# A hybrid decoder layer on one core: xBC, z and most gates as pairs of tiles in block products, with the scan between them

## The chip, the cores and the metric

The kernel runs on one core of a Trainium2 chip. Its engines work side by side, each on its own list of instructions in order: TensorE (matmuls), VectorE, ScalarE, GpSimd, and SyncE, which issues the DMAs. The metric is the device time of one execution in microseconds (us). Shorter is better.

## The reference, cut to what matters

All arrays are float32, x is 1024 tokens by 1024 channels, and one layer is computed.

```python
h = rms_norm(x, g_pre)
proj = jnp.einsum('bsd,dc->bsc', h, w_in)              # 1024 -> 12576 columns
(q, k, v, z_a, u, v_s, z_s, z_m, xbc, dt_raw, gate_logits) = jnp.split(proj, _split_points(), axis=-1)
y_att = sliding_window_attention(q, k, v, sinks, rel_bias) * jax.nn.silu(z_a)     # 16 heads of 64, window 128
y_sg = chunked_spatial_gate(u, v_s, sg_ln_g, sg_ln_b, sg_w, sg_b) * jax.nn.silu(z_s)
y_ssm = ssd_mixer(z_m, xbc, dt_raw, conv_w, conv_b, dt_bias, a_log, d_skip, ssm_norm_g)
gates = jax.nn.sigmoid(gate_logits.reshape(bsz, seq, N_BRANCHES, D_MODEL))
merged = gates[:, :, 0] * (y_att @ w_br_att) + gates[:, :, 1] * (y_sg @ w_br_sg) + gates[:, :, 2] * (y_ssm @ w_br_ssm)
return x + rms_norm(merged @ w_out, g_post)
```

The mixer `ssd_mixer` first runs a causal convolution of four taps and a silu over xbc (3072 channels: 2048 of x, 512 of B, 512 of C), and then, for each of 4 groups of 8 heads, a scan over 8 chunks of 128 tokens: inside a chunk, products of C and B weighted by decays; between chunks, a state of 128 by 512. Its output is multiplied by silu(z_m) (2048 channels) and normalised by group.

## The kernel before, in words

Each float32 operand of a large matmul is kept as a high and a low part, and three matmuls (high times high, high times low, low times high) make one product. A weight tile is loaded as `raw`, ScalarE rounds it to `whi`, VectorE subtracts to get `wlo` (`load_w`).

Most of the projection is made by `ct_unit`: one tile of 128 output channels for all 1024 tokens, in two halves of 512 tokens, each 8 steps over the input channels times three matmuls of 512 columns. `Stream.fill` puts pieces of such units into TensorE's order between the steps of other work; TensorE's order is the order of the program, the other engines' orders are set by a scheduler.

The stages are: the norm of x and a first unit; for each scan group g, six `conv_unit` tiles (xBC), then the 8 chunks of `Mix` with gate and z tiles as filler (from about 100 to 770 us); the attention with its q and z_a tiles; then u and z_s and twelve of the 24 gate tiles as pairs (to about 1400 us); the four quarters of the branch products (`br_unit`); and the output product.

The pairs are made by `PairStream`. It takes two tiles of output channels and the two halves of the tokens as a 2 by 2 block matrix, and makes it in seven block products in place of eight (twelve matmuls of 512 columns each). It needs sums of weight blocks (T1 to T4, on GpSimd, `ts`), sums of blocks of h (S1, S2 and S4, made once ahead of the stage), and sums of the products (u2, u3, u4 and the four output blocks, on VectorE out of PSUM and on GpSimd, `tp`). It prepares the operands of four products ahead.

A chunk in `Mix` has a part `local` (B and C and x of the chunk through TensorE; decays `seg`, `m` by ScalarE and VectorE), a part `scan` (the matmuls `po` with the state, `pn` for the new state, `pd` inside the chunk, then y on VectorE and GpSimd) and `sums`, which adds the squares of y over channels with a matmul. `decay` loads the decay rows two chunks ahead. The tiles xg, bc and z2 of a whole group stay in SBUF. The inverse norms of all chunks are made from `ssum` after the last group (a power on GpSimd, L622) and transposed after the units for k and q (L680).

In the branch stage `load_y` brings the y tiles back from DRAM; those of the first quarter wait for memory that the pairs' operands held.

## Time and profile before

| | |
|---|---|
| median of 3 runs | 1873.94 us (1871.6 to 1877.67) |
| the profiled execution's own time | 1872.69 us |
| its span, first to last instruction | 1871.0 us |
| mean granted TensorE clock | 0.988 |
| DMA | 192.85 MB, mean 103 GB/s |

The profile lists for each engine how long it was busy within the span, and for groups of instructions what ended the idle time in front of them. A wait of an engine that is not the bottleneck costs nothing by itself.

### The profile page before, as it was taken

Reading aid. Unit: us, or ns where it says so; the run is one execution under the profiler, and the core shown is the slowest. Engines: PE = TensorE matmul, PEld = TensorE weight load, DVE = VectorE, ACT = ScalarE, POOL = GpSimd, SP = SyncE. Lnnn points to the kernel's source line nnn. Section 1 sums busy time; section 2 is a strip of 40 time slices with the busy share of each in tenths; the row PEclk is TensorE's granted clock in tenths of the full one; section 3 lists DMA queues with packets and bytes.
Section 4 is the critical chain, followed back from the end, with each engine's and each line's share of the span. In section 5 each row is a group of like instructions: output and inputs, shape, how many; then the busy total and the mean of one; then the engine's idle time right before and its main releaser. Section 6 shows DMA issues by size and latency. Waiting matters only on the chain. (4 is left out here: it accounts for less than half of the span.)

```text
span 1871.0 us, 24800 instructions
## 1 busy us (share of the span) xinstructions
PE 1809.9 (97%) x9481; PEld 1529.9 (82%) x9481; DVE 1128.5 (60%) x1596; ACT 715.5 (38%) x1519; POOL 552.6 (30%) x552
## 2 busy tenths in 40 slices
PE   7999999999999999999999979999997999999998
PEld 6888778878878887888888978888885888888898
DVE  5446756675667557466666587766877243534424
ACT  5344454355436435356555433333233021212121
POOL 1000420240043015236665557554555200000000
PEclk9999999999999999999999989999998999999999
DMA  6211341342134124311111213322346453524303
GB/s 224 80 53 51 124 136 46 99 121 83 52 109 145 46 73 152 119 46 46 49 42 57 91 54 119 121 94 94 101 152 240 143 180 101 192 92 136 99 24 135
DMA packets 100662, 192.85 MB, mean 103 GB/s; under 512 B 9376, under 2 KB 55744, under 8 KB 100416
## 3 DMA queue, kind: packets, MB, share of 16 engines
q1 hardware_dynamic: 100544, 191.28, 31.5%
q8 instruction: 74, 1.21, 0.3%
q14 instruction: 44, 0.36, 0.1%
HBM read 152.83 MB, written 38.42 MB: 102 GB/s over the span
## 5 line engine op out<-in xcount | busy, mean ns | idle before, releaser
L106 PE MATMUL ps_mm<-h,whi 128*128 128x512 f32 x1104 | 436.3, 395 | 0.1
L108 PE MATMUL ps_mm<-h,wlo 128*128 128x512 f32 x1104 | 430.1, 390 | 0.0
L107 PE MATMUL ps_mm<-h,whi 128*128 128x512 f32 x1104 | 430.0, 389 | 0.0
L88 ACT CAST whi<-raw 128x1024 fp32r<-128x1024 f32 (+1 forms) x119 | 124.1, 1044 | 336.7 <-PE ps_mm L107 323.5
L108 PEld LDWEIGHTS ps_mm<-h,wlo 128*128 128x128 f32 x1104 | 207.2, 188 | 43.9
L106 PEld LDWEIGHTS ps_mm<-h,whi 128*128 128x128 f32 x1104 | 207.4, 188 | 43.5 <-issue 2.2
L107 PEld LDWEIGHTS ps_mm<-h,whi 128*128 128x128 f32 x1104 | 207.6, 188 | 40.7
L89 DVE TENSOR_TENSOR wlo<-raw,whi 128x1024 fp32r<-128x1024 f32 (+1 forms) x117 | 158.2, 1353 | 117.5 <-ACT whi L88 117.5
L106 PE MATMUL ps_mm<-y,whi 128*128 128x512 f32 x512 | 200.8, 392 | 11.1 <-ACT y L962 11.1
L107 PE MATMUL ps_mm<-y,whi 128*128 128x512 f32 x512 | 200.6, 392 | 2.0 <-DVE y L963 2.0
L108 PE MATMUL ps_mm<-y,wlo 128*128 128x512 f32 x512 | 200.1, 391 | 0.0
L552 POOL TENSOR_TENSOR y<-xg,dsk 128x512 f32<-128x512 f32 x32 | 40.5, 1276 | 390.0 <-issue 225.5
L493 DVE SCALAR_TENSOR_TENSOR acc<-xr,wcv,acc 128x512 f32<-128x512 f32 x144 | 111.4, 773 | 40.5 <-ACT acc L491 37.1
L106 PEld LDWEIGHTS ps_mm<-y,whi 128*128 128x128 f32 x512 | 96.9, 189 | 32.3 <-ACT y L962 11.9
L79 POOL TENSOR_TENSOR rso<-rso,mhalf_row 128x1 f32<-128x1 f32 x8 | 4.4, 552 | 401.0 <-DVE rso L78 401.0
L107 PEld LDWEIGHTS ps_mm<-y,whi 128*128 128x128 f32 x512 | 96.8, 189 | 23.1 <-DVE y L963 3.2
L985 DVE SCALAR_TENSOR_TENSOR tm<-gld,ps_mm 128x512 f32<-128x512 f32 x48 | 33.0, 687 | 134.6 <-PE ps_mm L108 134.6
L108 PEld LDWEIGHTS ps_mm<-y,wlo 128*128 128x128 f32 x512 | 96.8, 189 | 19.9
L131 PE MATMUL ps_mm<-whi,h 128*128 128x256 f32 (+1 forms) x256 | 81.6, 319 | 11.3 <-ACT whi L88 7.8
L528 ACT ACTIVATE seg<-seg,acs 128x128 f32<-128x128 f32 x256 | 80.4, 392 | 23.2 <-DMA seg<-acs_dr 22.2
L735 ACT ACTIVATE p<-s,mx 128x129 f32<-128x129 f32 x128 | 50.0, 392 | 96.3 <-DVE mx L731 96.3
L132 PE MATMUL ps_mm<-whi,h 128*128 128x256 f32 (+1 forms) x256 | 80.2, 313 | 1.8 <-DVE h L373 1.8
(236 smaller groups left out, 3753.8 us busy)
## 6 DMA issues: line engine op xcount, KB each, us to landing
seg<-acs_dr SPq DMA_DIRECT2D x32, 512.0 KB, 4.7
raw<-in_w_br_dram SPq DMA_DIRECT2D x32, 512.0 KB, 4.2
yraw<-y_dr SPq DMA_DIRECT2D x32, 512.0 KB, 5.3
gld<-gate_dr SPq DMA_DIRECT2D x32, 512.0 KB, 3.4
raw<-in_w_xbc_dram SPq DMA_DIRECT2D x24, 512.0 KB, 3.6
raw<-in_w_zm_dram SPq DMA_DIRECT2D x16, 512.0 KB, 3.5
y_dr<-y SPq DMA_DIRECT2D x32, 256.0 KB, 2.2
raw<-in_w_zu_dram SPq DMA_DIRECT2D x16, 512.0 KB, 3.5
```

The costliest lines, as they stand in the source:

```text
L88: A.copy(hi, raw)
L89: eng.tensor_tensor(lo, raw, hi.bitcast(F32), op=ALU.subtract)
L106: T.matmul(ps, lhsT=whi[:, ks], rhs=rhs(0, kt, half), start=kt == 0, stop=False)
L107: T.matmul(ps, lhsT=whi[:, ks], rhs=rhs(1, kt, half), start=False, stop=False)
L108: T.matmul(ps, lhsT=wlo[:, ks], rhs=rhs(0, kt, half), start=False, stop=kt == KT - 1)
L131: T.matmul(o, lhsT=lhs(0, kt, tt), rhs=whi[:, ks], start=kt == 0, stop=False)
L132: T.matmul(o, lhsT=lhs(1, kt, tt), rhs=whi[:, ks], start=False, stop=False)
L493: V.scalar_tensor_tensor(acc, xr[:, k + f0:k + f0 + 512], wcv[:, ti, k:k + 1], acc, op0=ALU.mult, op1=ALU.add)
L528: A.activation(seg[:, j, :], seg[:, j, :], AF.Relu, scale=-1.0, bias=acs[:, c, g * 8 + j:g * 8 + j + 1])
L552: G.tensor_tensor(d["y"], xg[g][:, :, cs], col(dsk, g), op=ALU.mult)
L735: A.activation(p[:, k, :], s4[:, k, :], AF.Exp, bias=mx[:, k:k + 1], accum_out=den[:, k:k + 1])
L985: V.scalar_tensor_tensor(tm, gt[0][:, fs], 1.0, ps, op0=ALU.add, op1=ALU.mult)
```

## The change

Attention comes first. Then one `PairStream` makes the xBC tiles (12 pairs), z (8 pairs), 22 of 24 gate tiles (11 pairs, one of them at the end) and the u and z_s tiles (8 pairs, as before). The scan's chunks stand between its products. As pairs come out of blocks and no longer stay for a whole group, the outputs go to DRAM (`x_dr`, `bc_dr`, `z_dr`), and each chunk loads its part. The convolution runs one block at a time, as a job after a product of the next unit. Within a chunk, VectorE's product of y and z, the state's decay and the sum of squares go to GpSimd; GpSimd's two scalings go to ScalarE, in four pieces. Buffers shrink: most tiles of a chunk have one buffer, and the decay rows of a chunk are loaded after the scan of the chunk before. The transpose of `ssum` moves to the end of the scan stage.

```diff
-NGATE = 12
+NGATE = 2
-ORDER = "zgzgzgzgzzzzg"
...
         def _prepare(self, q):
...
                 self._sum(b, "T3", "B22", "B12", ALU.subtract)
                 self._sum(b, "T2", "T3", "B11", ALU.add)
-                self._sum(b, "T1", "B12", "B11", ALU.subtract)
+                G.tensor_tensor(b["B12"], b["B12"], b["B11"], op=ALU.subtract)
+                b["T1"] = b["B12"]
+            elif i == 4:
                 self._sum(b, "T4", "T2", "B21", ALU.subtract)
...
             else:
-                block(11, V, t["s1"], o)
+                block(11, V, "s1", o)
+            if self.jobs and i in (1, 3, 4, 6):
+                self.jobs.pop(0)()
...
+    def z_pair(g, n):
+        def evac(b, d):
+            d = d[:, 4:]
+            th = ap.tile([P, 512], F32, name="acc", bufs=3)
+            A.activation(th, d, AF.Tanh, scale=0.5)
+            V.scalar_tensor_tensor(d, th, 1.0, d, op0=ALU.add, op1=ALU.mult)
+            store(z_dr, g, b // 10 - 1, 2 * n + b % 10 - 1, d)
...
+        def conv(half, k, d):
...
+            A.activation(acc, body, AF.Identity, scale=wcv[:, ti, 3:4], bias=bcv[:, ti:ti + 1])
+            for tap in range(3):
+                V.scalar_tensor_tensor(acc, d[:, 1 + tap:513 + tap], wcv[:, ti, tap:tap + 1], acc,
+                                       op0=ALU.mult, op1=ALU.add)
+            silu2(body, acc)
+            if n < 2:
+                store(x_dr, g, half, 2 * n + k, body)
+            else:
+                store(bc_dr, g, half, k, body)
...
+                if c + 1 < NB:
+                    if c == 0:
+                        A.copy(state, pn)
+                    else:
+                        G.tensor_tensor(v8(state), v8(state), hb(etot, c, g), op=ALU.mult)
+                        V.tensor_tensor(state, state, pn, op=ALU.add)
+                V.tensor_tensor(y, y, v4(pd), op=ALU.add)
+                if c > 0:
+                    G.tensor_tensor(y, y, t1, op=ALU.add)
+                G.tensor_tensor(y, y, self.z, op=ALU.mult)
+                sq = mp.tile([P, 4, P], F32, name="t1")
+                A.activation(sq, y, AF.Square)
+                for j in range(4):
+                    A.activation(y[:, j, :], y[:, j, :], AF.Copy, scale=ng[:, g * 4 + j:g * 4 + j + 1])
+                G.tensor_tensor(sq[:, 0:2, :], sq[:, 0:2, :], sq[:, 2:4, :], op=ALU.add)
+                self.ss = mp.tile([P, P], F32, name="ssy")
+                G.tensor_tensor(self.ss, sq[:, 0, :], sq[:, 1, :], op=ALU.add)
...
+        group(0, "xxzxz")
+        for g in range(4):
+            group(g + 1, "xzxzxgg" if g < 2 else "xzxzxg" if g == 2 else "ggggg")
+            if g == 0:
+                pst.run(33)
+            mix = Mix(g)
+            mix.load_x(0)
+            mix.load_a(0)
+            pst.run(2)
+            for c in range(NB):
+                mix.load_z(c)
+                mix.local(c)
+                if c + 1 < NB:
+                    mix.load_x(c + 1)
+                pst.run(4)
+                if pst.done % 7 in (3, 6):
+                    pst.run(1)
+                if c > 0:
+                    mix.sums(c - 1)
+                mix.scan(c)
+                if c + 1 < NB:
+                    mix.load_a(c + 1)
+                    pst.run(1)
+            pst.run(2)
+            mix.sums(NB - 1)
+            while pst.done < 7 * len(pst.units) - (2 if g < 3 else 0):
+                pst.run(1)
+
+        V.tensor_scalar(ssum, ssum, 1.0 / 2048.0, EPS, op0=ALU.mult, op1=ALU.add)
+        G.tensor_tensor(ssum, ssum, mhalf.broadcast_to([P, 32]), op=ALU.pow)
+        rt = mp.tile([32, P], F32, name="ssy")
+        ps = psum(ps_tr, "tr")
+        T.transpose(ps[0:32, 0:P], ssum, ident)
...
     def load_y(n, eng=V):
-        raw = py.tile([P, S], F32, name="yraw", bufs=4)
+        raw = (py if n % 4 < 2 else pz).tile([P, S], F32, name=f"yraw{n % 4 // 2}", bufs=2)
         nc.sync.dma_start(out=raw, in_=y_dr[n])
...
-    pst.run(3)
     st.add(*br[:8])
     st.loaded = st._load()
     pst.run(4)
```

The order of VectorE's instructions in one chunk of the scan before (group 3), from the chunk's first to its last; L89 is the low part of a whole weight tile, which comes now and then between chunks:

```order
L543 TENSOR_TENSOR gtm<-ps_tr,gmask 128x128
L545 COPY btok<-ps_tr 128x128
L547 TENSOR_TENSOR xdt<-ps_tr,dth 128x512
L553 TENSOR_TENSOR seg<-seg,gtm 128x1024
L582 SCALAR_TENSOR_TENSOR t_5746<-ps_ac,ea 128x512
L578 TENSOR_TENSOR st<-st,ps_ac 128x512
L583 TENSOR_TENSOR y<-y,ps_ac 128x512
L577 TENSOR_TENSOR st<-st,etot 128x512
L586 TENSOR_TENSOR y<-y,z_4358 128x512
L590 TENSOR_REDUCE ssy<-sqj 128x128
```

The same engine in chunk 1 of group 0 of the changed kernel, from inside the chunk (L818 is the second half of its decays) to where its three operations on the scan's results begin (L839, L845, L846); L237 is a low part, L271 an output block of a pair, L723 a conv operation, L341 a silu:

```order
L818 TENSOR_TENSOR seg<-seg,gtm 128x512
L341 SCALAR_TENSOR_TENSOR tp<-tp,acc 128x512
L237 TENSOR_TENSOR wlo<-raw,whi 128x512
L237 TENSOR_TENSOR wlo<-ts,whi 128x512
L271 TENSOR_TENSOR tp<-tp,ps_mm 128x512
L723 SCALAR_TENSOR_TENSOR acc<-tp,wcv,acc 128x512
L738 COPY tp<-tp 128x3
L237 TENSOR_TENSOR wlo<-raw,whi 128x512
L723 SCALAR_TENSOR_TENSOR acc<-tp,wcv,acc 128x512
```

Between the scan's own operations now stand low parts, output blocks, conv operations and silus: 31 instructions from one chunk to the next in place of 10. GpSimd in the same two places, before (an xde, the y scalings and the sum of y and t):

```order
L585 TENSOR_TENSOR y<-y,t_5841 128x512
L550 TENSOR_TENSOR xde<-xdt,edec 128x512
L591 TENSOR_TENSOR y<-y,ng 128x512
L552 TENSOR_TENSOR y<-xg,dsk 128x512
L585 TENSOR_TENSOR y<-y,t_5942 128x512
```

and in the changed kernel from one chunk's state decay (L844) to the next one's (L216, L228: sums of weight blocks; L273, L283: sums of products):

```order
L844 TENSOR_TENSOR st<-st,etot 128x512
L848 TENSOR_TENSOR y<-y,t_6279 128x512
L849 TENSOR_TENSOR y<-y,zch 128x512
L216 TENSOR_TENSOR ts<-ts,raw 128x512
L216 TENSOR_TENSOR ts<-raw 128x512
L854 TENSOR_TENSOR t_6286<-t_6286 128x256
L228 TENSOR_TENSOR raw<-raw 128x512
L856 TENSOR_TENSOR ssy<-t_6286 128x128
L808 TENSOR_TENSOR xde<-xdt,edec 128x512
L216 TENSOR_TENSOR ts<-ts,raw 128x512
L283 TENSOR_TENSOR tp<-tu,tp 128x512
L273 TENSOR_TENSOR tp<-tp 128x512
```

A chunk of GpSimd grows from four operations to twelve: the sums for the pairs, the state's decay, the product with z and the squares come in, the two scalings go. Last, TensorE at the end of the scan, before; L596 is the sum of squares of the last chunk, and gate tiles follow it:

```order
L107 MATMUL ps_mm<-h_98,whi 128x512
L108 MATMUL ps_mm<-h_97,wlo 128x512
L596 MATMUL ps_tr<-ones,ssy 128x1
L106 MATMUL ps_mm<-h_99,whi 128x512
L107 MATMUL ps_mm<-h_100,whi 128x512
```

and after the change, from the part `local` of the last chunk (L792 to L796) to the transpose of `ssum` (L904) and the first matmul of the next product (L259); L861 are the sums, L828 and L835 the matmuls `po` and `pd`:

```order
L792 MATMUL ps_tr<-bcch 128x128
L793 MATMUL ps_tr<-ident,bcch 128x128
L796 MATMUL ps_tr<-ident,xch 128x128 x4
L861 MATMUL ps_tr<-mhalf_row,ssy 128x1
L828 MATMUL ps_ac<-cT,st 128x128 x4
L835 MATMUL ps_ac<-seg,xdt 64x128 x8
L861 MATMUL ps_tr<-mhalf_row,ssy 128x1
L904 MATMUL ps_tr<-ident,ssum 32x128
L259 MATMUL ps_mm<-h_104,whi 128x512
```

The last chunk and the transpose stand together with no product between them; the products of z_s and u come behind.

## Rows read from the trace of the kernel before

**Rows 1.** The page: span, and busy time of each engine.

```profile
span 1871.0 us, 24800 instructions
...
PE 1809.9 (97%) x9481; PEld 1529.9 (82%) x9481; DVE 1128.5 (60%) x1596; ACT 715.5 (38%) x1519; POOL 552.6 (30%) x552
```

**Rows 2.** Waits of TensorE, whole span: total us, times, longest us.

```profile
PE ps_mm L106 <- ACT y L962: 11.1, 2, 6.9
PE ps_tr L596 <- DVE btok L545: 10.9, 4, 3.2
...
PE ps_mm L131 <- ACT whi L88: 7.8, 1, 7.8
```

**Rows 3.** Busy time in five stretches, granted clock, DMA share, GB/s.

```profile
core 0: us, PE busy (x) PEld busy (x) DVE busy (x) ACT busy (x) POOL busy (x), PEclk, DMA share, GB/s
100.00:770.00 670.00, 656.26 (x3408) 532.70 (x3407) 430.56 (x591) 301.48 (x600) 158.19 (x121) 0.99 0.30 93
1080.00:1100.00 20.00, 11.73 (x79) 11.23 (x78) 17.20 (x19) 7.52 (x15) 15.82 (x10) 0.74 0.17 53
1120.00:1380.00 260.00, 259.33 (x1221) 216.70 (x1220) 191.98 (x245) 86.25 (x155) 139.21 (x95) 1.00 0.33 105
1400.00:1450.00 50.00, 36.91 (x145) 28.94 (x144) 36.18 (x25) 16.28 (x18) 28.19 (x11) 0.86 0.65 224
1450.00:1500.00 50.00, 50.00 (x222) 41.39 (x222) 12.31 (x15) 4.57 (x5) 10.44 (x4) 1.00 0.39 134
```

**Rows 4.** Timeline of one scan chunk, TensorE and ScalarE: start, duration.

```profile
220.81 2.45 ACT L528 ACTIVATE seg<-seg,acs 128x128 f32<-128x128 f32 x8 [0.33 <-DMA seg<-acs_dr]
221.02 0.38 PE L537 MATMUL ps_tr<-bc 128*128 128x128 f32 x2
...
224.15 1.06 ACT L530 ACTIVATE seg<-seg 128x1024 f32<-128x1024 f32 x1
...
225.28 0.49 PE L537 MATMUL ps_tr<-bc 128*128 128x128 f32 x2
```

**Rows 5.** Timeline of VectorE among the block products.

```profile
1307.16 0.68 DVE L227 TENSOR_TENSOR wlo<-ts,whi 128x512 fp32r<-128x512 f32 x1
1307.76 0.68 DVE L227 TENSOR_TENSOR wlo<-raw,whi 128x512 fp32r<-128x512 f32 x1
...
1326.01 1.72 DVE L874 SCALAR_TENSOR_TENSOR zs<-th,zs 128x512 f32<-128x512 f32 x1 [0.76 <-ACT th L873]
...
1328.38 0.68 DVE L261 TENSOR_TENSOR zs<-tp,ps_mm 128x512 f32<-128x512 f32 x1
```

**Rows 6.** Timelines of GpSimd: the scan, then the block products.

```profile
725.71 1.04 POOL L550 TENSOR_TENSOR xde<-xdt,edec 128x512 f32<-128x512 f32 x1
...
1325.89 1.29 POOL L209 TENSOR_TENSOR ts<-ts,raw 128x512 f32<-128x512 f32 x1
1327.14 0.74 POOL L886 TENSOR_SCALAR_AFFINE_SELECT sgw<-sgw 128x128 f32<-128x128 f32 x1
```

**Rows 7.** Groups by line: count, busy us, mean ns, idle before.

```profile
L227 DVE TENSOR_TENSOR wlo<-ts,whi 128x512 fp32r<-128x512 f32 x56 | 51.4, 934 | 4.0 <-ACT whi L226 3.8
...
L209 POOL TENSOR_TENSOR ts<-raw 128x512 f32<-128x512 f32 x28 | 42.3, 1512 | 41.1 <-DVE wlo L227 40.3
...
L493 DVE SCALAR_TENSOR_TENSOR acc<-xr,wcv,acc 128x512 f32<-128x512 f32 x144 | 111.4, 773 | 40.5 <-ACT acc L491 37.1
```

**Rows 8.** DMA issues: count, KB each, median us to landing.

```profile
seg<-acs_dr SPq DMA_DIRECT2D x32, 512.0 KB, 4.7
...
yraw<-y_dr SPq DMA_DIRECT2D x32, 512.0 KB, 5.3
...
y_dr<-y SPq DMA_DIRECT2D x32, 256.0 KB, 2.2
```

**Rows 9.** Timeline after the last chunk's sum of squares.

```profile
768.33 0.28 PE L596 MATMUL ps_tr<-ones,ssy 128*128 128x1 f32 x2
...
769.02 0.15 ACT L597 COPY ssum<-ps_tr 128x1 f32<-128x1 f32 x1
...
769.21 0.18 DVE L621 TENSOR_SCALAR ssum<-ssum 128x32 f32<-128x32 f32 x1 [4.29 <-ACT ssum L597]
769.47 5.44 POOL L622 TENSOR_TENSOR ssum<-ssum,mhalf_row 128x32 f32<-128x32 f32 x1 [6.20 <-DVE ssum L621]
```

More of the change, by code (lines that the diff above doesn't have):

```diff
@@ L207, in _sum @@
         def _sum(self, b, out, x, y, op):
-            b[out] = self.pool.tile([P, 512], F32, name="ts", bufs=3)
+            b[out] = self.pool.tile([P, 512], F32, name="ts", bufs=2)
             G.tensor_tensor(b[out], b[x], b[y], op=op)
@@ L408, in hybrid_kernel @@
             _, run = tc_unit(None, h_tc, first_evac, 416, mid=first_pre)
-            st.add(*[z_unit(0, j) for j in range(4)])
+            st.add(vs_unit(1))
             for _ in run(wfirst):
@@ L420, in hybrid_kernel @@
             nc.sync.dma_start(out=bcv, in_=t["conv_b"])
+            ones = xp.tile([P, P], F32, name="ones")
+            V.memset(ones, 1.0)
             tri = xp.tile([P, P], F32, name="tri")
@@ L599, in hybrid_kernel @@
-        gates = iter(range(24))
-        for g in range(4):
-            st.add(*[conv_unit(g, j) for j in (4, 5, 0, 1, 2, 3)])
-            st.drain()
-            mix = Mix(g)
-            st.add(*[gate_unit(next(gates), mp) for _ in range(6 if g == 3 else 2)])
-            if g < 3:
-                st.add(*[z_unit(g + 1, j) for j in range(4)])
-            mix.decay(0)
-            st.fill(10.4)
-            for i in range(NB + 3):
-                if i < NB:
-                    mix.local(i)
-                    if i + 1 < NB:
-                        mix.decay(i + 1)
-                st.fill(2.2)
-                if 3 <= i:
-                    mix.sums(i - 3)
-                if 1 <= i <= NB:
-                    mix.scan(i - 1)
-                st.fill(2.2)
@@ L678, in hybrid_kernel @@
         st.add(za_unit(0))
-        ps = psum(ps_tr, "tr")
-        T.transpose(ps[0:32, 0:P], ssum, ident)
-        rt = ac.tile([32, P], F32, name="rt")
-        A.copy(rt, ps[0:32, 0:P])
-        nc.sync.dma_start(out=rs_dr, in_=rt)
         bias = ac.tile([P, 16, P], F32, name="bias")
@@ L794, in hybrid_kernel @@
                     else:
-                        st.add(*[vs_unit(qd) for qd in range(1, 4)])
+                        st.add(*[vs_unit(qd) for qd in range(2, 4)], *[gate_unit(i) for i in range(NGATE)])
             st.fill(2.6)
@@ L841, in hybrid_kernel, with gate_pair @@
             split(hB[1, 0], kt, made[kt][2])
+    vsp_open.close()
+    ep = es7.enter_context(tc.tile_pool(name="ep", bufs=1, side="right", reuse_waits="tile"))
+    ap_open = ExitStack()
+    ap = ap_open.enter_context(tc.tile_pool(name="ap", bufs=1, side="right", reuse_waits="tile"))
+    pst = PairStream(ep, lambda i, part, kt: blocks[i][part][:, kt, :])
+    def gate_pair(n):
+        def evac(b, d):
+            d = d[:, 4:]
+            A.activation(d, d, AF.Tanh, scale=0.5)
+            i, half = NGATE + 2 * n + b % 10 - 1, b // 10 - 1
+            nc.sync.dma_start(out=gate_dr[i, :, half * 512:(half + 1) * 512], in_=d)
+        return [t["w_gp"][n][k] for k in range(2)], evac
@@ new lines, in chunks, with store, evac @@
+    def chunks(dr, g, half, j):
+        return dr[g, half * 4:(half + 1) * 4, :, j, :].rearrange("c p l -> p c l")
+    def store(dr, g, half, j, d):
+        nc.sync.dma_start(out=chunks(dr, g, half, j), in_=d.rearrange("p (c l) -> p c l", c=4))
+    def z_pair(g, n):
+        def evac(b, d):
+            d = d[:, 4:]
+            th = ap.tile([P, 512], F32, name="acc", bufs=3)
+            A.activation(th, d, AF.Tanh, scale=0.5)
+            V.scalar_tensor_tensor(d, th, 1.0, d, op0=ALU.add, op1=ALU.mult)
+            store(z_dr, g, b // 10 - 1, 2 * n + b % 10 - 1, d)
+        return [t["w_zm"][2 * g + n][k] for k in range(2)], evac
```

395 lines of the change are left out of this document (186 added, 209 removed).

## The prediction

> **What bounds the kernel now.** I read the page first: TensorE is busy 97% of the span, VectorE 60%, ScalarE 38%, GpSimd 30% [rows 1]. The reader is to see that on average nothing but TensorE is near its limit. Its longest waits are few; those before L596 in the scan, on VectorE, and those at the start of the branch stage, before L106 on ScalarE, matter here [rows 2]. Then the stages: from 100 to 770 us, where xBC, z and the first gates are made and the scan runs, TensorE is idle for 670.0 - 656.3 = 13.7 us; from 1120 to 1380 us, the block products, for 0.7 us, with VectorE busy 192 of 260 us [rows 3]. A stretch with nothing but 512-column matmuls has 222 of them in 50 us, so one costs 0.2252 us [rows 3] (its own duration of 0.39 us overlaps with the next).
>
> **What is removed.** A tile of 128 output channels by itself takes 2 halves x 8 x 3 = 48 such matmuls, a pair of tiles in seven block products 7 x 12 = 84 in place of 96. The change pairs 24 more tiles of xBC, 16 of z and 10 of the gates: 25 pairs x 12 x 0.2252 = **67.6 us** off TensorE. The old scan stage goes, and with it its 13.7 us of waits. The scan's own matmuls (4.4 us a chunk, from L537 at 221.02 to L537 at 225.28, with a weight load ahead [rows 4]) stay the same in number and shape. Of these 81 us, what isn't saved has to turn up as new waits.
>
> **What is added.** A block product (2.70 us of TensorE) needs a half-width low part on VectorE; seven of them need five sums out of PSUM there and six sums on GpSimd. An xBC pair adds twelve conv and four silu operations, a z pair four. Between the products now run 32 scan chunks. In a chunk the change takes the state's decay and the product with z from VectorE and gives them to GpSimd, and the sum of squares too; two scalings go from GpSimd to ScalarE.
>
> Prices. On VectorE, back to back, a 128x512 operation starts 0.60 us after the last [rows 5]; a conv operation, which needs the one before it, takes 0.77 on average [rows 7]; I use 0.72, as the new order puts others between some of them. A GpSimd sum starts the next 1.25 us later (1325.89 to 1327.14), one with a broadcast operand takes 1.04 [rows 6]. These are times without disturbance; the means among the block products are 0.93 and 1.51 [rows 7]. The timeline says why: the VectorE operation at 1326.01 reads two SBUF tiles, takes 1.72 us, and ends 0.55 us after the GpSimd sum of 1325.89 has ended at 1327.18; the one at 1328.38, with one operand in PSUM, takes 0.68 [rows 5, 6]. So a VectorE operation on two SBUF tiles and a GpSimd one don't overlap here; one waits for the whole of the other. The Trainium skill (SBUF — State Buffer, Who interferes with whom) states this as an exclusive lock between just these two kinds, and speaks against a change that puts more work on both engines at once: by it the undisturbed prices of the two add up, as in the sum below; by the mean prices they do not, as in rival (a).
>
> Take the heavy stretch of each of the first three groups: chunks 0 to 6, with the next group's xBC and z pairs between them. The changed program has 36 products there (group 0). TensorE: 36 x 2.70 + 7 x 4.4 = 128 us. VectorE on two SBUF tiles: 36 low parts (21.8), 30 conv (21.6), 19 silu and z (11.5), 14 half-width decays (8.4): 63 us. VectorE out of PSUM: 25 sums and 26 scan operations at 0.605, 14 small ones at 0.2: 34 us. GpSimd: 31 sums at 1.25, and in the scan 13 operations at 1.04, 13 at 1.25, and 0.6 + 0.3 a chunk: 75 us. If GpSimd worked in all the time that VectorE spends on PSUM or waiting, the stretch would take 63 + 75 = 138 us; if never, 63 + 34 + 75 = 172.
>
> How much overlaps is read from 1120 to 1380 us: 13 units, 8 of them pairs of z_s and u. By the same prices VectorE has 91 low parts, 48 other half-width operations (0.64) and 8 of full width (1.2) on two SBUF tiles, 95 us, and 65 sums, 16 mixed outputs and 8 small ones out of PSUM, 52 us; it is busy 192, so it was blocked for 45. GpSimd has 78 sums and 8 times 2.25 us, 116 us, of which 116 - 45 = 71 lay beside VectorE's 52 of PSUM work and 68 of idleness: 59% of those. With this share, and 6 us of other waits (a buffer of block sums is free only when its store has landed; conversions on ScalarE), VectorE is blocked in the heavy stretch for 75 - 0.59 x 40 = 51 us, and the stretch takes 97 + 51 + 6 = 154. GpSimd has more queued here, which raises the share a little; I take 153, 25 us over TensorE's 128: **+75 us** for the three (bounds +30 and +132).
>
> The head, 35 products before the first chunk, by the same sum: VectorE 59 + 15, GpSimd 37.5, blocked 25, other waits 6: 105 against 94.5; I take **+9**. The tails with gates only (13, 13 and 8 products with a chunk each), the last group's first chunks, and the pairs of z_s and u hold TensorE's time above the others' sum: nothing.
>
> The end of the scan is new. In the last group the products run out: one stands before the last chunk but one and one inside it, none in the last chunk, and TensorE then has the transpose of all sums of squares ahead of any product of z_s and u. A chunk's decay rows are asked for only when the chunk before has read its own: issue 0.5, landing 4.7 [rows 8], ScalarE 2.45 + 1.06 [rows 4], VectorE 0.6: 9.3 us, against 2.7 + 1.2 + 2.7 of TensorE's work in the last chunk but one (2.7 idle) and 1.2 in the last (8.1 idle). Then the last chunk's chain: VectorE 0.7, GpSimd 1.25 twice, ScalarE 0.6, GpSimd 0.9, TensorE 0.3, ScalarE 0.15, VectorE 0.2, and the power on GpSimd, 5.44 us [rows 9]: 10.8, with handovers 12. Before, the products of k and q stood between these sums and the transpose. All of TensorE's later work is queued behind it. **+23 us** (bounds 12 and 30).
>
> The branch stage starts with 13.1 us of idleness now (1400 to 1450 us [rows 3]), when y tiles wait for their memory. After the change the raw buffers of tiles 2 and 3 lie in the late pool, so they can't be loaded ahead, and four products instead of seven cover the first two. A landing of 5.3 us [rows 8] comes onto the path: **+5 us** (0 to 10).
>
> Costed at nothing: ScalarE's conversions, silus and scalings, some 100 us a stretch at 0.3 (eight in 2.45 us [rows 4]) to 0.6, are covered while a stretch is longer. The detour through DRAM is 80 stores and 96 loads, 41 MB, on top of a mean DMA share of 0.30 [rows 3]; a store (2.2 us [rows 8]) and a load have 8 or more products of cover. Were it late, a chunk's transposes would wait, and all products behind them.
>
> **Sum.** -67.6 - 13.7 + 75 + 9 + 23 + 5 = +30.7 us on an execution of 1872.7 (the span of 1871.0 and 1.7 around it): 1903.4. The median of the runs is 1.2 above that execution: **1905 us**.
>
> **The rivals.** (a) TensorE stays the bound: blocking costs an operation no more than now. By the means [rows 7] VectorE needs 36 x 0.93 + 30 x 0.77 + 19 x 1 + 8.4 + 34 = 118 of 128 us, the 75 and the 9 fall away, 23 + 5 remain, and 3 for small waits: 1873.9 - 81.3 + 31 = **1824**, faster. For it: 1120 to 1380 us, where VectorE at 74% busy cost TensorE nothing. Against it: GpSimd has 75/36 = 2.1 us of work per product in a stretch, there 1.3, and what it has more must block more. It decides if a stretch stays at 128 us. (b) GpSimd always has work ready, 138 us a stretch: +30 and +4 in place of 75 and 9, **1855**; between that and 146 a stretch the time ends at or under 1879. Against it: GpSimd works in order, and in each chunk waits for VectorE's sum and ScalarE's square. (c) TensorE's waits grow long enough for its clock to fall, as from 1080 to 1100 us, granted 0.74 on average around a wait of 7.8 us for L88 [rows 2, 3]. A chunk with five products at 1.2 GHz takes 31 us, over VectorE's 22; a fall that costs 3 us in 12 of 24 chunks gives **1941**. Against it: the scan's waits now reach 3.2 us at most [rows 2]. (d) The end of the scan is hidden by work I don't see: **1882**.
>
> **How the numbers follow.** A difference under 0.3% (5.6 us) is about what a measurement of this kernel can't tell from none. Chances: my forecast with (d) 0.50, (a) 0.18, (b) 0.20, (c) 0.12. Faster: (a) and 0.14 of (b), 0.32; the same: the rest of (b) and 0.04 of the forecast, 0.10; slower 0.58. The forecast's own range is 1880 to 1930. To leave out no more than 2 in 10, with half of (a) and half of (c) outside, the range goes from 1826 to 1940.
>
> **What would show it.** Right: TensorE idle for 15 to 20% of the heavy stretches, its waits ended by VectorE (low parts, block sums); low parts at 1 us or more on average and VectorE over 90% busy there; two idle pieces of some 8 and 12 us at the end of the scan, the second ended by GpSimd's power. Wrong: TensorE over 97% busy in those stretches (a); stretches of 140 us with GpSimd rarely idle (b); a granted clock under 0.95 over the stage (c). The weakest step is the share of 59%, read from a stage with another mix of operations.

## The result, and the profile after

The changed kernel takes **1948.87 us** (median of 4 runs, 1946.59 to 1954.24), the kernel before 1872.77 in the same session: a ratio of 1.041, interval 1.037 to 1.045. It is slower, as forecast, but by 76 us in place of 31, and outside the range. The profiled execution took 1947.21 us; my sum for it was 1903.4, so 43.8 us have to be found.

The page, to be held against [rows 1]:

```profile
span 1945.5 us, 25952 instructions
...
PE 1779.0 (91%) x9181; PEld 1496.0 (77%) x9181; DVE 1287.3 (66%) x1815; ACT 846.8 (44%) x1966; POOL 819.8 (42%) x759
```

TensorE's busy time fell by 30.9 us, though 300 matmuls at 0.2252 are 67.6: 36.7 us went into the matmuls that were left, with a granted clock of 0.957 over the span against 0.988 before. Its idle time rose from 61.1 to 166.5 us. By stages, cut at the first transposes of a chunk (L792): the head, then a heavy stretch and a tail for each of three groups, the last group, and the end of the scan (columns as in [rows 3]).

```profile
429.10:530.85 101.75, 98.08 (x421) 79.65 (x422) 95.95 (x126) 49.33 (x92) 48.23 (x31) 0.98 0.36 108
530.85:684.76 153.91, 131.16 (x668) 105.24 (x667) 128.62 (x179) 91.96 (x222) 90.95 (x68) 0.93 0.49 147
684.76:734.63 49.87, 41.03 (x193) 33.72 (x192) 32.92 (x46) 28.16 (x66) 25.60 (x20) 0.90 0.49 149
734.63:882.48 147.85, 130.70 (x668) 104.94 (x667) 116.99 (x167) 87.56 (x212) 84.97 (x66) 0.94 0.46 139
882.48:935.03 52.55, 42.52 (x193) 34.28 (x192) 35.56 (x48) 29.40 (x67) 26.86 (x21) 0.90 0.49 149
935.03:1084.01 148.98, 131.27 (x668) 105.48 (x667) 120.69 (x167) 87.74 (x212) 89.40 (x68) 0.94 0.46 139
1084.01:1120.27 36.26, 27.44 (x132) 22.52 (x131) 26.26 (x36) 22.51 (x56) 20.07 (x17) 0.86 0.56 163
1120.27:1246.34 126.07, 115.11 (x585) 92.66 (x584) 70.84 (x102) 70.48 (x177) 71.80 (x61) 0.95 0.49 154
1246.34:1277.65 31.31, 13.43 (x83) 10.10 (x82) 13.39 (x30) 17.20 (x49) 20.02 (x17) 0.66 0.34 101
```

| piece | predicted, us | measured, us | difference |
|---|---|---|---|
| head, 35 products | 103.5 | 101.8 | -1.7 |
| three heavy stretches | 3 x 153 | 450.7 | -8.3 |
| three tails (13, 13, 8 products) | 39.5 + 39.5 + 26 | 138.7 | +33.7 |
| last group and end of scan (33 products, 8 chunks, and 23) | 147.3 | 157.4 | +10.1 |
| branch start to end of span | before + 5 | before + 12.6 | +7.6 |

The last row goes from the first matmul of the branch products to the end: 464.9 us before, 477.5 after. The differences come to 41.4 of the 43.8 us. What TensorE waits for, against [rows 2] (total, times, longest):

```profile
PE ps_ac L259 <- DVE t L839: 65.3, 14, 8.6
PE ps_tr L861 <- POOL ssy L856: 36.1, 5, 8.8
...
PE ps_tr L904 <- POOL ssum L901: 6.0, 1, 6.0
```

The first row: a product wants one of the three PSUM banks that hold a chunk's results, and VectorE has not yet read the first of them (L839). Why VectorE is late is in the timelines of such a wait. TensorE:

```profile
572.60 0.76 PE L259 MATMUL ps_ac<-S,whi 128*128 128x512 f32 x1 [8.55 <-DVE t L839]
```

VectorE in that time (L723 are convolution steps, L341 is a silu), with L839 as its last row:

```profile
565.31 3.43 DVE L723 SCALAR_TENSOR_TENSOR acc<-tp,wcv,acc 128x512 f32<-128x512 f32 x2
568.66 0.68 DVE L280 TENSOR_TENSOR tu<-tp,ps_mm 128x512 f32<-128x512 f32 x1
569.25 1.15 DVE L341 SCALAR_TENSOR_TENSOR tp<-tp,acc 128x512 f32<-128x512 f32 x1
570.33 1.52 DVE L723 SCALAR_TENSOR_TENSOR acc<-tp,wcv,acc 128x512 f32<-128x512 f32 x1
571.77 0.68 DVE L839 SCALAR_TENSOR_TENSOR t<-ps_ac,ea 128x512 f32<-128x512 f32 x1
```

And GpSimd:

```profile
564.75 1.76 POOL L216 TENSOR_TENSOR ts<-raw 128x512 f32<-128x512 f32 x1 [1.85 <-DMA raw<-in_w_xbc_dram]
566.59 1.59 POOL L216 TENSOR_TENSOR ts<-ts,raw 128x512 f32<-128x512 f32 x1
568.14 1.71 POOL L228 TENSOR_TENSOR raw<-raw 128x512 f32<-128x512 f32 x1
569.82 1.48 POOL L844 TENSOR_TENSOR st<-st,etot 128x512 f32<-128x512 f32 x1
```

While GpSimd makes its sums, two convolution steps on SBUF tiles take 3.43 us, and a third takes 1.52 beside the state's decay (L844); L280, with an operand in PSUM, takes 0.68 in the midst of a GpSimd sum. L839 stands behind them in order. After 8.55 us of waiting TensorE's matmul takes 0.76 us instead of 0.39. The means of such operations from 531 to 1080 us:

```profile
L723 DVE SCALAR_TENSOR_TENSOR acc<-tp,wcv,acc 128x512 f32<-128x512 f32 x102 | 95.4, 943 | 6.4 <-ACT acc L721 6.2
L237 DVE TENSOR_TENSOR wlo<-raw,whi 128x512 fp32r<-128x512 f32 x76 | 80.0, 1060 | 11.0 <-ACT whi L236 10.7
```

The second row of the waits stands in the tails, for instance here: the scan of the group's last chunk is issued, VectorE comes to its first result 8 us later, and TensorE waits for the sum of squares that GpSimd makes at the end of that chain.

```profile
697.64 1.09 PE L835 MATMUL ps_ac<-seg,xdt 128*64 128x128 f32 x16
...
706.92 0.68 DVE L839 SCALAR_TENSOR_TENSOR t<-ps_ac,ea 128x512 f32<-128x512 f32 x1
...
713.26 0.58 PE L861 MATMUL ps_tr<-mhalf_row,ssy 128*128 128x1 f32 x2 [8.84 <-POOL ssy L856]
```

### The profile page after: what moved, and what is told of

Read it like the earlier page. It is cut to its first block, busy times and chain, and to the rows that moved or that the text cites. A ratio compares the mean times of both kernels' runs of the same rounds, so it can differ in the third digit from the quotient of the medians.

```text
span 1945.5 us, 25952 instructions
## 1 busy us (share of the span) xinstructions
PE 1779.0 (91%) x9181; PEld 1496.0 (77%) x9181; DVE 1287.3 (66%) x1815; ACT 846.8 (44%) x1966; POOL 819.8 (42%) x759
## 4 chain that ended last, share of the span: by engine, by line
PE 49%; DVE 17%; POOL 11%; issue 10%; ACT 8%; DMA 4%; SPq 0%; POOLq 0%; DVEq 0%; ACTq 0%
PE ps_mm L114 7%; PE ps_mm L113 7%; PE ps_mm L115 7%; PE ps_mm L259 4%; PE ps_mm L260 4%; PE ps_mm L261 4%; DVE acc L723 3%; PE ps_mm L139 3%; PE ps_mm L138 3%; PE ps_mm L140 3%; POOL ts L216 2%; DVE wlo L237 2%; PE ps_ac L259 2%; POOL y L849 2%; PE ps_ac L260 2%
## 5 line engine op out<-in xcount | busy, mean ns | idle before, releaser
L216 POOL TENSOR_TENSOR ts<-ts,raw 128x512 f32<-128x512 f32 x78 | 120.2, 1541 | 174.6 <-DVE wlo L237 168.8
L259 PE MATMUL ps_mm<-h,whi 128*128 128x512 f32 x468 | 189.0, 404 | 4.9 <-DVE tp L271 3.1
L261 PE MATMUL ps_mm<-h,wlo 128*128 128x512 f32 x468 | 185.7, 397 | 0.0
L260 PE MATMUL ps_mm<-h,whi 128*128 128x512 f32 x468 | 185.6, 396 | 0.0
L95 ACT CAST whi<-raw 128x1024 fp32r<-128x1024 f32 (+1 forms) x69 | 71.7, 1041 | 255.7 <-PE ps_mm L114 238.1
L237 DVE TENSOR_TENSOR wlo<-raw,whi 128x512 fp32r<-128x512 f32 x156 | 157.3, 1016 | 16.8 <-ACT whi L236 16.4
L723 DVE SCALAR_TENSOR_TENSOR acc<-tp,wcv,acc 128x512 f32<-128x512 f32 x144 | 134.4, 943 | 7.2 <-ACT acc L721 6.9
L237 DVE TENSOR_TENSOR wlo<-ts,whi 128x512 fp32r<-128x512 f32 x117 | 109.0, 931 | 24.6 <-ACT whi L236 22.9
L259 PE MATMUL ps_mm<-S,whi 128*128 128x512 f32 x312 | 124.1, 398 | 0.5 <-DVE tp L271 0.5
L113 PE MATMUL ps_mm<-h,whi 128*128 128x512 f32 x304 | 121.7, 400 | 2.0 <-ACT vst L324 2.0
L260 PE MATMUL ps_mm<-S,whi 128*128 128x512 f32 x312 | 121.8, 390 | 0.0
L261 PE MATMUL ps_mm<-S,wlo 128*128 128x512 f32 x312 | 121.7, 390 | 0.0
L115 PE MATMUL ps_mm<-h,wlo 128*128 128x512 f32 x304 | 119.4, 393 | 0.0
L114 PE MATMUL ps_mm<-h,whi 128*128 128x512 f32 x304 | 119.1, 392 | 0.0
```

What stands on the lines that cost most here:

```text
L95: A.copy(hi, raw)
L113: T.matmul(ps, lhsT=whi[:, ks], rhs=rhs(0, kt, half), start=kt == 0, stop=False)
L114: T.matmul(ps, lhsT=whi[:, ks], rhs=rhs(1, kt, half), start=False, stop=False)
L115: T.matmul(ps, lhsT=wlo[:, ks], rhs=rhs(0, kt, half), start=False, stop=kt == KT - 1)
L216: G.tensor_tensor(b[out], b[x], b[y], op=op)
L237: V.tensor_tensor(lo, src, hi.bitcast(F32), op=ALU.subtract)
```

## The experiments

**Theory A**: GpSimd's reading of SBUF and VectorE's work on two SBUF tiles exclude each other, and this sets the stretches. **B**: the engines wait for one another in order (ScalarE for GpSimd's product with z, then VectorE, then TensorE). **C**: the lower clock. A fourth: only the place of the sums of squares makes the tails long. Edits are against the changed kernel, times medians; the kernel before took 1873 to 1876 us beside them. In the shorter runs the window of the last column reaches into the last group.

| run | us | heavy stretches | tails | low parts of raw blocks, 531 to 1080 us, ns |
|---|---|---|---|---|
| changed kernel | 1948.9 | 153.9, 147.9, 149.0 | 49.9, 52.6, 36.3 | 1060 |
| late_sums | 1938.6 | 155.1, 160.5, 154.8 | 44.0, 38.8, 30.9 | 1092 |
| late_square | 1931.9 | 157.5, 147.4, 151.7 | 40.6, 42.9, 36.0 | 1063 |
| no_weight_sums | 1878.1 | 136.7, 137.9, 136.9 | 46.8, 46.4, 33.7 | 844 (all) |
| own_bank | 1949.4 | 149.1, 146.1, 146.1 | 51.4, 52.2, 40.2 | 1056 |
| sums_on_vector | 1917.3 | 145.6, 143.6, 143.6 | 47.8, 50.4, 33.2 | 891 |
| pool_copies | 1916.6 | 144.7, 144.2, 144.2 | 50.0, 50.1, 36.3 | 952 |
| pool_memsets | 1890.8 | 140.9, 137.4, 136.3 | 47.3, 46.8, 34.5 | 869 |
| end_filled | 1933.1 | 153.5, 147.7, 149.0 | 49.8, 52.5, 36.3 | 1074 |
| conv_in_psum | 1920.4 | 148.3, 149.5, 148.9 | 40.7, 45.2, 25.6 | 1017 |
| warm_clock | 1997.8 | 166.8, 165.2, 162.0 | 48.5, 53.2, 35.3 | 1052 |
| combined | 1880.4 | 145.5, 148.1, 146.7 | 38.8, 39.5, 25.6 | 932 |
| combined_vector | 1875.4 | 147.4, 144.7, 143.2 | 38.8, 38.8, 28.1 | 885 |
| own_conv_bank | 1908.7 | 136.1, 136.7, 136.1 | 49.5, 51.2, 35.1 | 990 |
| combined_own_bank | 1862.5 | 131.3, 134.2, 130.3 | 43.5, 43.1, 39.4 | 905 |
| combined_vector_own_bank | 1851.9 | 140.1, 133.6, 133.3 | 39.8, 41.6, 33.3 | 863 |
| vector_no_conv | 1870.2 | 135.3, 138.3, 135.6 | 43.5, 45.3, 35.6 | 840 |

**late_sums.** The last sums of a group come later.

```diff
-            pst.run(2)
+            pst.run(8)
             mix.sums(NB - 1)
```

> In the changed kernel three tails of gate products take 49.9, 52.6 and 36.3 us where I had costed them at 39.5, 39.5 and 26; TensorE's five waits for GpSimd's sums of squares come to 36.1 us, and the last sums of a group stand only two products behind its last chunk. Here they stand eight behind it for the first three groups. Theory (the place of these sums makes the tails long): the waits of the sums fall under 10 us, the tails to 40 to 43, 40 to 43 and 27 to 30 us, and the kernel to 1915 to 1925 us. Rival (the engines behind the products are late there anyway, and the sums only show it): the wait moves to the products' own lines, and the time stays within 8 us of 1949.

The tails lost 25 us and the stretches took 20 of them back. The kernel is 10 us shorter, but 3 of these lie ahead of the first chunk, where nothing was moved: the place of the sums is worth 5 to 10 us, less than a third of the tails. Neither forecast was met: the waits for the sums fell to 22.0 us, not under 10, and the wait for L839 rose from 65.3 to 69.1. So most of the wait only moved, as if VectorE's and GpSimd's unfinished work had to be waited for in one stretch or another.

**late_square.** The end of scan() becomes a function of its own, called before the next scan.

```diff
+            def finish(self):
+                g, (c, y) = self.g, self.pend
                 sq = mp.tile([P, 4, P], F32, name="t1")
                 A.activation(sq, y, AF.Square)
...
                 if c > 0:
+                    mix.finish()
+                mix.scan(c)
+                if c > 0:
                     mix.sums(c - 1)
-                mix.scan(c)
```

> Nothing is left out. The square, the two scalings, GpSimd's sums of squares and the store of a chunk are written down one chunk later, so that ScalarE does not stand at the square waiting for GpSimd's product with z (114.5 us in 29 waits in the changed kernel); the sums of a chunk move behind the next chunk's scan, the last ones of a group seven products behind it. Theory B (the engines are late because they wait for one another in order, ScalarE first): the heavy stretches fall from 148 to 154 us to 133 to 140, and with the tails mended as in the run with late sums the kernel comes to 1870 to 1890. Theory A (the exclusive use of SBUF by VectorE and GpSimd sets the stretch, the waits only fill the time): the stretches stay within 4 us, and the time is that of the run with late sums, 1915 to 1925.

1931.9: 7 us better than late_sums, the stretches 2 us longer on average, far from B's 1870 to 1890 (A's 1915 to 1925 was missed with late_sums; its stretches within 4 us came true). But the edit took little of what it was made for: ScalarE still waits 95.3 us in 21 waits for GpSimd's product with z, against 114.5 in 29. So this run hardly tests B; the runs that change what GpSimd does and keep the order do.

**no_weight_sums.** L216 and L228 fall away.

```diff
-            if i == 1:
-                self._sum(b, "T3", "B22", "B12", ALU.subtract)
...
-            src = b[("B11", "T2", "T1", "T3", "B22", "T4", "B21")[i]]
+            src = b[("B11", "B22", "B12", "B12", "B22", "B21", "B21")[i]]
```

> GpSimd's four sums of weight blocks per pair are left out and raw blocks are used in their place, so the outputs of the pairs are other numbers; everything else stays. That takes 21 sums of 1.25 us, 26 us, from GpSimd in a heavy stretch. Theory A (work on two SBUF tiles of VectorE and GpSimd adds up): by the prediction's sum a stretch is 97 + 75 - 26 - 0.59 x 40 + 6 = 129 us, that is TensorE's own 128 to 133, in place of 150; low parts fall to 0.75 us on average or less; the kernel comes to 1880 to 1895. Theory B (waits in order between chunk work of ScalarE, GpSimd and VectorE): the stretches lose 5 us each at most, 1930 or more.

The groups of VectorE from 531 to 1080 us (count, busy, mean ns, idle before):

```profile
L229 DVE TENSOR_TENSOR wlo<-raw,whi 128x512 fp32r<-128x512 f32 x148 | 122.7, 844 | 31.8 <-ACT whi L228 31.4
L715 DVE SCALAR_TENSOR_TENSOR acc<-tp,wcv,acc 128x512 f32<-128x512 f32 x108 | 90.8, 849 | 3.2 <-ACT acc L713 2.9
```

The kernel is 71 us shorter without these sums: A's time (1880 to 1895) or a little better, 52 us under B's. The stretches went to 137, not 129, and the low parts, all of raw blocks now, to 844 ns (in the changed kernel all together 1.00 us), where an undisturbed one takes 0.68 and starts 0.60 after the last [rows 5]. That the other GpSimd work still blocks them would fit; it was not taken away.

**own_bank.**

```diff
-            o = psum(ps_ac, "ac") if i in (2, 5) else psum(ps_mm, "mm")
+            o = psum(ps_mm, "mm")
```

> Nothing is left out. The third and sixth product of a pair take their PSUM bank from the three of the other products and no longer from the three that the scan's results use. In the changed kernel TensorE's largest wait, 65.3 us in 14 waits, is for such a bank, freed by VectorE's reading of the scan's first result. Theory (the shared banks are the cause): this wait goes, the kernel gets 30 to 60 us shorter, 1890 to 1920. Rival (VectorE is late anyway; the bank is where it shows): the wait turns up before the scan's matmuls, before the chunk's transposes or before other products, TensorE's idle time in the heavy stretches stays within 5 us of 58, and the time within 10 of 1949.

The 65 us of waits are gone from the list, and the time is the same, as the rival said; in their place stand, below the first row, waits of the same products for other readers of PSUM:

```profile
PE ps_tr L861 <- POOL ssy L856: 40.5, 7, 8.4
PE ps_mm L259 <- DVE tp L271: 18.4, 14, 3.2
PE ps_mm L259 <- ACT tp L277: 16.9, 7, 3.7
PE ps_mm L259 <- DVE tu L280: 14.6, 7, 3.0
PE ps_mm L259 <- ACT tp L282: 11.6, 5, 2.7
```

The stretches themselves did get 9 us shorter in sum, but the tails 5 longer (the first row was 36.1), the last group 3, and the time up to the first chunk 5. So for the kernel the largest row of the list of waits was a symptom. The first two stretches (columns as in [rows 3]):

```profile
536.16:685.24 149.08, 132.43 (x669) 103.65 (x667) 124.62 (x175) 90.85 (x221) 89.93 (x67) 0.97 0.48 147
...
736.60:882.70 146.10, 132.37 (x668) 104.00 (x668) 116.13 (x167) 86.89 (x212) 84.08 (x66) 0.96 0.47 141
```

The granted clock rose to 0.96 and 0.97 from 0.93 and 0.94, but TensorE's busy time did not fall (131.2 and 130.7 in the changed kernel): the gain is idle time, not faster matmuls. That is the first evidence against C.

**sums_on_vector, pool_copies, pool_memsets.** The same four sums per pair, three ways.

```diff
-            G.tensor_tensor(b[out], b[x], b[y], op=op)
+            V.tensor_tensor(b[out], b[x], b[y], op=op)          # sums_on_vector
+            for _ in range(2): G.tensor_copy(b[out], b[y])      # pool_copies
+            for _ in range(2): G.memset(b[out], 0.01)           # pool_memsets
```

The fourth sum, L228, is changed in the same way.

> Nothing is left out: the four sums of weight blocks per pair move from GpSimd to VectorE. Theory A (work on two SBUF tiles of the two engines adds up): a sum costs VectorE 0.62 us and cost GpSimd 1.25, so VectorE goes to 97 + 13 = 110 us in a heavy stretch, GpSimd to 49, blocked 49 - 0.59 x 40 = 25, other waits 6: 141 us a stretch in place of 150, and the kernel 1890 to 1925 us, although the busier of the two gets more work. Rival (VectorE's own queue sets the stretch, whatever GpSimd does): 13 us more for it in each of three stretches and the head, 1975 to 1995.

> Each of GpSimd's four sums of weight blocks per pair is replaced by two copies of one block, so the outputs of the pairs are other numbers. GpSimd still reads SBUF; if two copies take about the time of a sum, theory A (reading SBUF by GpSimd excludes a VectorE operation on two SBUF tiles) expects the changed kernel's time, 1930 to 1960, low parts at 0.95 us or more on average. Beside it stands the run in which GpSimd writes only.

> Each of GpSimd's four sums of weight blocks per pair is replaced by two memsets of the same tile, so the outputs of the pairs are other numbers. GpSimd's queue stays occupied and the tiles change hands as before, but these instructions read nothing. The Trainium skill (SBUF - State Buffer, Who interferes with whom) has a VectorE instruction with two SBUF inputs contend with GpSimd's reading alone, not with a GpSimd instruction that only writes. Theory A with that rule: low parts at 0.86 us or less, stretches of 141 us or less, the kernel at 1865 to 1895, as without the sums. Rival (GpSimd's queue as such, the order of waits): 1920 or more, low parts as with the copies.

With the sums VectorE, the busier engine, has 156 instructions more, and the kernel is 32 us shorter, at 144 us a stretch (141 by the sum), 58 us under the rival's nearest time. Over the whole span a GpSimd sum of the changed kernel takes:

```profile
L216 POOL TENSOR_TENSOR ts<-ts,raw 128x512 f32<-128x512 f32 x78 | 120.2, 1541 | 174.6 <-DVE wlo L237 168.8 <-DMA raw<-in_w_zu_dram 4.7 <-DMA raw<-in_w_zm_dram 0.7
```

GpSimd's groups over the whole span and VectorE's low parts from 531 to 1080 us, with copies, then with memsets:

```profile
L217 POOL COPY ts<-raw 128x512 f32<-128x512 f32 x234 | 199.0, 851 | 201.5 <-DVE wlo L239 177.8 <-ACT acc L710 6.3 <-ACT whi L238 5.6
...
L239 DVE TENSOR_TENSOR wlo<-raw,whi 128x512 fp32r<-128x512 f32 x79 | 74.7, 952 | 11.8 <-ACT whi L238 11.5
```

```profile
L217 POOL MEMSET ts<- 128x512 f32 x234 | 123.1, 527 | 217.1 <-DVE wlo L239 211.0
...
L239 DVE TENSOR_TENSOR wlo<-raw,whi 128x512 fp32r<-128x512 f32 x84 | 72.6, 869 | 14.6 <-ACT whi L238 14.2
```

Memsets keep GpSimd occupied for 1.05 us per sum and cost 13 us against no sums at all; copies, which read, take 1.70 and cost 39. That agrees with the rule that a GpSimd instruction which only writes does not contend (the Trainium skill, SBUF — State Buffer, Who interferes with whom), though the copies also last longer, so the two are not a pure pair. I had expected the copies to be as bad as the sums (1930 or more), and they were not: 1916.6 with more GpSimd time. Why two short readings cost less than one long sum isn't settled, and theory A in its plain form doesn't say it.

**end_filled.** Five products of z_s and u stand inside the last group, two more before the transpose of the sums.

```diff
+            if g == 3:
+                pst.add(zu_unit(0))
...
-                pst.run(4)
+                pst.run(4 if g < 3 else 3)
```

> Nothing is left out. The first five products of z_s and u are made inside the last group: one product less per chunk there, so that some are left for the last chunk and for the time behind it, and the transpose of all sums of squares comes after two further products. The prediction put 23 us on the end of the scan. If that is right, the stretch from the last group's first chunk to the products of z_s and u loses 15 to 22 us, less the five products of 2.7 us that it takes over, and the kernel comes to 1927 to 1934. Rival (the last group waits in the same way with fewer products per chunk, the time only moves): 1942 or more.

1933.1. From the last group's first chunk to that transpose it took 161.1 us with 7 more products (18.9 us): 142.2 against 157.4, 15 us saved, as forecast. The term of 23 us for the end was right in kind, and most of it can be had back.

**conv_in_psum, own_conv_bank.** To own_bank's edit comes that the convolution's accumulator goes into a PSUM bank, first one of the scan's three, then one of its own; the scan keeps two, and its third result goes to the products' banks.

```diff
-            acc = ap.tile([P, 512], F32, name="acc", bufs=3)
+            acc = psum(ps_ac, "ac")      # conv_in_psum
+            acc = psum(ps_cv, "cv")      # own_conv_bank
...
-                pd = psum(ps_ac, "ac")
+                pd = psum(ps_mm, "mm")   # own_conv_bank
```

> Nothing is left out. The run with products in their own banks, and in addition the convolution's accumulator lies in one of the three other PSUM banks, so that its three steps and the silu read one SBUF tile and one PSUM tile; VectorE issues as many instructions as before, GpSimd too. Theory A (only a VectorE operation on two SBUF tiles and GpSimd's reading exclude each other): 28 us of VectorE's work in a heavy stretch leave that class, blocked 75 - 0.59 x 68 = 35 us, the stretch 97 + 35 + 6 = 138 us in place of 146 to 149, conv steps at 0.75 us or less on average in place of 0.96, the kernel 1905 to 1925. Rival (it is the amount of work, or TensorE now waits for banks that the convolution holds): conv steps stay above 0.85, or TensorE waits before the scan's matmuls, 1940 or more.

> Nothing is left out. The changed kernel with the convolution's accumulator in a PSUM bank that nothing else of this stage uses (attention's values use it before), two banks for the scan's first two results, and the third result and all products in the three others. With the accumulator in the scan's banks the kernel took 1920 us, its stretches 148 to 150, and TensorE waited 45 us before the scan's matmuls. If the shared banks are the new wait: no wait before the scan's matmuls over 3 us, stretches of 138 to 143, the kernel 1890 to 1908. Rival (the stretch's rest is order and contention): the waits move to the products, stretches of 146 or more, 1913 or more.

Of the first, the convolution's group from 531 to 1080 us, and then TensorE's waits (total, times, longest):

```profile
L723 DVE SCALAR_TENSOR_TENSOR ps_ac<-tp,wcv,ps_ac 128x512 f32<-128x512 f32 x108 | 79.3, 747 | 3.5 <-ACT ps_ac L721 3.2
```

```profile
PE ps_ac L831 <- DVE tp L341: 24.2, 6, 6.4
...
PE ps_ac L835 <- issue: 20.9, 3, 7.5
```

The convolution is out of the contention (747 ns, 943 in the changed kernel), the tails are 32 us shorter than own_bank's, but the stretches stay at 149 where A's sum was 138. The kernel came out in A's range, with the rival's waits: the first row is the scan waiting for a bank that a silu of the convolution still reads; for the second the profile names no releaser. With a bank of its own the stretches are 136 us (138 by the sum of A), the waits before the scan's matmuls come to 1.1 us, and the kernel is 0.7 us above its forecast. The tails are then long again; waits for GpSimd's sums of squares come to 27.0 us.

**warm_clock.**

```diff
+            if i in (2, 5) and self.warm:
+                self.warm = False
+                idle = psum(ps_tr, "tr")
+                for _ in range(16):
+                    T.matmul(idle, lhsT=self.lhs(0, 0, 0)[:, 0:P], rhs=self.lhs(0, 0, 1), start=True, stop=True)
```

> Nothing is left out; 16 matmuls whose result nobody reads (3.6 us at full clock) stand before the first product that needs one of the scan's PSUM banks, after each of 28 scan chunks, where TensorE waited 65 us in 14 waits. They tell the clock apart from the waits. Rival C of the prediction (the waits lower the clock, and the slow matmuls behind them make the kernel longer): granted clock 0.97 or more in the heavy stretches, and the kernel 15 us or more shorter, under 1934. Theory A (VectorE and GpSimd set the stretch; the slow matmuls lie in time that TensorE has to spare): the clock rises as well, the idle time of the stretches is filled, but they do not get shorter; 1945 to 1975, the longer the more chunks had no wait.

The clock rose (0.95 and 0.96 in the stretches, 1.00 in two of the tails and in the last group), and the kernel became 49 us longer, beyond both. The instrument had a wait of its own:

```profile
PE ps_tr L259 <- DVE btok L805: 36.2, 10, 8.1
```

The idle matmuls stood waiting for a transpose bank. In the stretches 80 of them (18 us) each were made, and the stretches grew by 13 to 17 us: they did not go into the idle time. So the run says nothing about C.

**combined, combined_vector, vector_no_conv, combined_own_bank, combined_vector_own_bank.** late_square, late sums and end_filled together, the masked product left in PSUM (below; the sums of squares then use the same bank), and with or without weight sums on VectorE and convolution in PSUM.

```diff
-                gt = mp.tile([P, P], F32, name="gtm")
-                V.tensor_tensor(gt, pg[:, 0:P], gmask, op=ALU.mult)
+                self.pg, gt = pg, pg[:, 0:P]
+                V.tensor_tensor(gt, gt, gmask, op=ALU.mult)
```

> Nothing is left out. Late square and late sums, the filled end of the scan, the convolution's accumulator in PSUM, and the masked B by C product left in PSUM too, so that the eight decay products per pair of halves have one SBUF operand. Theory A: 36 us of VectorE's work in a stretch have left the class that GpSimd excludes; blocked 75 - 0.59 x 76 = 30, stretch 97 + 30 + 6 = 133; with 16 us from the end and 15 from the tails the kernel comes to 1855 to 1890. Rival (TensorE waits for PSUM banks in place of VectorE's SBUF work): 1900 or more.

> The combined kernel with the four weight sums per pair on VectorE as well; nothing is left out. Theory A: VectorE 110 us a stretch, GpSimd 49, blocked at most 49 - 0.59 x 76 = 4, so that 120 us lie under TensorE's 128 to 131, and TensorE bounds the stretch: 1835 to 1870. Rival (VectorE at 85% of a stretch is late in its order even undisturbed): stretches of 138 us or more, 1880 or more.

> Nothing is left out. The combined kernel with the weight sums on VectorE, but with the convolution's accumulator back in SBUF. If convolution in PSUM with shared banks gives as much as it takes: 1870 to 1885. If the contention that it removes is worth more than its waits: 1890 to 1905.

> Nothing is left out. The combined kernel (1880 us) with the convolution's own PSUM bank. If the shared banks hold its stretches at 146 to 148: stretches of 133 to 140, the kernel 1845 to 1865, shorter than the kernel before the change. Rival: within 6 us of 1880.

> Nothing is left out. The combined kernel with the weight sums on VectorE (1875 us) and the convolution's own PSUM bank. If the shared banks hold its stretches at 143 to 147: stretches of 131 to 137, the kernel 1835 to 1858. Rival: within 6 us of 1875.

Both with shared banks only reached the kernel before (ratios 1.004, interval 1.002 to 1.005, and 1.001, 1.000 to 1.002), their stretches held at 143 to 148 by the banks, where A's sums were 133 and TensorE's own 128 to 131; without convolution in PSUM it was 1870 (0.999, 0.997 to 1.001). With the bank of its own they took 1862.5 (0.994, 0.993 to 0.996) and **1851.9 us (0.989, 0.985 to 0.993): shorter than both kernels**, 97 us under the changed one. Its page and three of its stages:

```profile
span 1850.2 us, 25831 instructions
...
PE 1757.9 (95%) x9181; PEld 1479.0 (80%) x9181; DVE 1270.8 (69%) x1971; ACT 843.7 (46%) x1966; POOL 574.1 (31%) x603
```

```profile
709.21:842.83 133.62, 127.62 (x668) 102.29 (x667) 118.82 (x187) 86.31 (x210) 56.10 (x46) 0.99 0.53 159
842.83:884.44 41.61, 39.41 (x192) 32.29 (x191) 37.59 (x58) 30.02 (x71) 14.88 (x12) 1.00 0.60 176
884.44:1017.71 133.27, 127.57 (x668) 102.19 (x667) 115.99 (x191) 87.22 (x211) 53.62 (x46) 0.99 0.54 159
```

TensorE is within 6 us of its own 128 in these two stretches, at a granted clock of 0.99; the first took 140.1 us.

## Why the prediction was wrong, point by point

- **What is removed**, 67.6 and 13.7 us: the matmuls went as counted (9481 to 9181), but TensorE's busy time fell only by 30.9.
- **The heavy stretches, +75**: right in size, 150.2 us on average against 153, and in the kind of wait: TensorE was idle for 12 to 15% of them (15 to 20 forecast), 53.9 of these 57.6 us for L839 on VectorE; low parts took 1.06 us (of raw blocks). But two terms of the sum were off in opposite directions, so part of the agreement is luck. Of the 51 us for which I had VectorE blocked, 20 to 32 are there (busy 117 to 129 us, 97 by my prices), and it stood without work for 25 to 31 us in place of 6, busy for 79 to 84% and not over 90. GpSimd was busy for 85 to 91 us against 75: it was held up too. no_weight_sums, pool_memsets, sums_on_vector and own_conv_bank moved as the sum says, within 8 us a stretch; conv_in_psum, combined and combined_vector missed it by 11 to 14. The share of 59% is not confirmed by this, and VectorE's idle time may be waits of theory B's kind: no run takes it away.
- **The tails and the last group's first chunks at nothing** is the step that failed. The tails are 33.7 us over it, 27.7 of them idle time and 25.6 of that one wait per tail for the sums of squares (8.8, 8.0 and 8.8). I compared engine sums in each tail by itself. But VectorE enters a tail with the last xBC pair's convolution still to do (seven or eight steps and three silus), and the sums of the last chunk stand only two products behind its scan. From that scan to its sums the prediction's own prices give 4.7 us, under the two products; in the first tail it took 14.5, of which VectorE needed 8 to come to L839. late_sums shows that the place of the sums is worth 5 to 10 us; the rest moves into the next stretch, so stretch and tail have one budget: 196 us a group measured on average, 188 by my two terms together. What sets that budget is argued from the runs, not shown by one. The last group's first six chunks, with 32 products, took 126.1 us where the same prices give 112.8; 11.0 of the 13.3 us are waits for L839.
- **The end**, +23: 3 us too large. There were two idle pieces, but the first was 4.9 us, not 8, and it waited for the sums of squares of the chunk before, not for decay rows; the second was 5.5 and 6.0 us, as forecast, its last part for GpSimd's power.
- **The branch start**, +5: measured +12.6. 4.6 us are idle time, as said. 5.0 us are slow matmuls: the first 50 took 20.8 us of busy time in place of 15.8. The other 2.9 us lie behind the last matmul of the kernel, where VectorE now waits 1.5 to 1.7 us for each of the last loads of x. The stretch from 1450 to 1500 us, to be held against the fourth of [rows 3]:

```profile
1450.00:1500.00 50.00, 32.04 (x116) 23.05 (x115) 25.89 (x21) 13.96 (x16) 21.52 (x10) 0.75 0.61 211
```

- **The head**, +9: 7 measured.
- **Rival (c)**, 1941, lies nearest to the time, and its sign is there: a granted clock of 0.93 in the stretches, 0.90 in the tails, matmuls of 0.76 us after long waits. But it isn't what makes the stretches long: own_bank raised the clock and TensorE's busy time stayed, and in a stretch the slow matmuls come to 3 to 4 us (131 busy, 127.6 for as many at 0.99 in combined_vector_own_bank) beside 17 to 23 idle. How much of the 36.7 us lengthened the kernel is open. **(a)** is wrong: prices did not stay at their old means (low parts of raw blocks 1.06 us, convolution steps 0.94 in place of 0.77). **(b)** asked for stretches of 138 us with GpSimd hardly idle; it was busy for 57 to 60% of them. **(d)** fell with end_filled.

## What to carry to other kernels

Budget GpSimd's SBUF reading together with VectorE's work on two SBUF tiles: where both stand between matmuls, as here, moving elementwise work to the slower helper can cost more than leaving it on the busy engine (32 us here), and an operand in PSUM took an operation out of the contest; only a bank of its own kept TensorE from waiting for it. Budget a stage together with the one behind it, since work that is late is paid where cover runs out. The longest row in a list of waits may name only where lateness shows: take that wait away and see whether the time goes with it.
